# The order of TensorE's instructions behind the input projection, written in the source instead of planned

## Chip, cores and metric

The kernel runs on one core of one Trainium2 chip. The metric is the time of one execution on the device in microseconds (us), as the median of several runs; one more execution was recorded by the hardware profiler, and every row of the trace comes from that one.

## What is computed

One decoder block on 1024 tokens of width 1024, in float32. The state-space branch works in 8 chunks of 128 tokens, one after the other, because each chunk needs the state that the chunk before it left.

```
h = layer_norm(x)
xs, z, b, c, dt, glu, cgate = split(h @ w_in)            # 44 blocks of 128 columns, and dt
...
# state-space branch: 16 heads x 64, 2 groups, state 128, chunks of 128 tokens
y[chunk]  = (c b^T * decay) @ (x * dt)  +  c @ state * exp(cumsum)  +  d_skip * x
state     = state * chunk_decay  +  b^T @ (x * dt * decay_to_end)
y_ssm     = rms_norm(y * silu(z)) * ssm_norm_g
# convolution branch
y_conf    = silu(layer_norm(conv31(glu))) * silu(cgate)
out       = concat(y_ssm, y_conf) @ w_out
h1        = layer_norm(alpha * h + out + b_out)
result    = layer_norm(alpha * h1 + sigmoid(h1 @ w_ple_gate) * (p @ w_ple_proj))
```

## The kernel before

Every large matrix product is made of three passes: an operand is split into a rounded high part and the low rest (`split`, lines 117 to 120: ScalarE writes the high part, VectorE or GpSimd subtracts), and `three` (lines 122 to 125) issues low x high, high x low, high x high for each 128 rows of the contraction. So a line number of 123, 124 or 125 alone says little; the name of the output tile says which product it is: `ps` is the input projection, `pso` the output projection of the convolution branch, `pss` that of the state-space branch, `psg` the last gate.

The program has three stretches. In the first, the blocks of the input projection run (`inproj`), each in two halves of 24 matmuls: the blocks of the convolution branch, then those of x, B, C and z (`xbc_tile`, `z_tile`, the list `others`), then the norm over channels (`conf_norm`), the 8 gate blocks (`gate_tile`) and, behind them, the last two z blocks. Results that are needed by chunk go to memory (`xbc_d`, `z_d`, `mix_d`) and are read again.

In the second stretch the 8 chunks of the scan and the output projection of the convolution branch alternate. For chunk c, `prep` loads its inputs, takes the exponentials on ScalarE, turns x (`xtok`) and B and makes C B^T (`bps`) on TensorE, and weights them on VectorE. `chunk` does what needs the state (`yo`), what lies inside the chunk (`yd`) and the new state (`sp`), and gates with z on GpSimd. `mean_square` squares (ScalarE), adds up (GpSimd) and sums over channels with four tiny matmuls (`pr`). `conf_out` adds 48 matmuls (`pso`) to the residual. Meanwhile `out_weight` loads and splits the weights `wc` (convolution branch), `ws` (state-space branch) and `wg` (gate).

In the third stretch, for each 128 tokens, `out_proj` makes 48 matmuls (`pss`), a residual sum and a layer norm on VectorE and GpSimd, giving `r`; `turned` turns `r` with eight transposes (`pt`) and splits it into `hTH` and `hTL`; `gate` makes 48 matmuls (`psg`) from them, first of all one that reads `hTL`. The loop in the source is

```
    ready, last = out_proj(0, *ys.pop(0)), None
    for c in range(NT):
        if c + 2 < NT:
            ys.append(y_load(c + 2))
        following = out_proj(c + 1, *ys.pop(0)) if c + 1 < NT else None
        now = last or turned(c, ready)
        ahead = turned(c + 1, following) if c + 2 == NT else None
        gate(c, ready, *now)
        ready, last = following, ahead
```

What sets the order of the instructions on an engine: a planner (`schedule_with_timeline_sim=True`). It goes through a simulated execution and gives each engine, whenever it is free there, the instruction that is ready and stands earliest in the source. So the order of the source is a priority, and a later piece may overtake an earlier one that isn't ready. At run time each engine executes its list in that order; waits are semaphores. Tiles come from pools: a tag has a number of buffers (`BUFS`, lines 67 and 147), and a tile waits until a buffer of its tag comes free. Those that matter here are `y` (2 buffers: the last z blocks' results `zt`, the raw weights k = 3 and k = 7 of `wc`, and each chunk's `y`), `xb` (2: the inputs of a chunk), `E` and `M` (4 each, first held by the low part of the input of the input projection, which its last block still reads). In PSUM, `s` has 3 banks, `o` has 2, `b` one, and `cv` (with `xtok` and `pt`) one pair. All transfers are issued on SyncE's queue.

Of the kernel before, what the change touches and what calls it, by code (L numbers as in the profile page):

```python
# [46 lines left out]
def tile_block(ctx: ExitStack, tc: tile.TileContext, x, pT, wple, win, wdt, wout, wgate, vec, rows, heads, out):  # L47
    nc = tc.nc
    mm = nc.tensor.matmul

# [108 lines left out]
    def embed(half):  # L159
        for t in range(half * 4, half * 4 + 4):  # L160
            mu, rs = moments(xts[t], "0")
            if t in NORM_ACT:
                nm = small("nm0", 1)
                nc.gpsimd.tensor_scalar(out=nm, in0=mu, scalar1=rs, scalar2=-1.0, op0=ALU.mult, op1=ALU.mult)
                nc.scalar.activation(out=xts[t], in_=xts[t], func=AF.Identity, scale=rs, bias=nm)
            else:
                nc.vector.tensor_scalar(out=xts[t], in0=xts[t], scalar1=mu, scalar2=rs, op0=ALU.subtract, op1=ALU.mult)
        for k in range(NK):
            ps = obank("pst")
            for i in range(4):  # L170
                nc.tensor.transpose(out=ps[:, i * P:(i + 1) * P], in_=xts[half * 4 + i][:, k * P:(k + 1) * P], identity=ident)
            if k % 2 == 0:
                both = work("htmp", "ha" if k == 4 else "gt")
            tmp = both[:, k % 2 * 512:k % 2 * 512 + 512]
            nc.scalar.activation(out=tmp, in_=ps, func=AF.Identity, scale=v("lng", k), bias=v("lnb", k))
            hs = slice(half * 512, half * 512 + 512)
            nc.vector.tensor_copy(out=hH[k][:, hs].bitcast(F32R), in_=tmp)  # L177
            leng = nc.gpsimd if k in L_POOL else nc.vector
            leng.tensor_tensor(out=hL[k][:, hs].bitcast(F32R), in0=tmp, in1=hH[k][:, hs], op=ALU.subtract)  # L179
# [173 lines left out]
    def decays():  # L353
# [9 lines left out]
        psr = obank("psr")  # L363
        nc.tensor.transpose(out=psr[:, 0:P], in_=nacs, identity=ident)
        nc.vector.tensor_scalar(out=ar, in0=psr[:, 0:P], scalar1=-1.0, scalar2=None, op0=ALU.mult)
# [74 lines left out]

    def prep(c):

# [3 lines left out]
        for g in range(2):  # L446
# [3 lines left out]
            gg.append(gt)  # L450
        ea = slabs(work("ea", "u") if c == 0 else area("ea", "E"))
        for q in range(2):
            er = ea_d[c * HEADS:(c + 1) * HEADS, :].rearrange("(t q) l -> q t l", q=2)[q]
            nc.sync.dma_start(out=ea[q * HD:(q + 1) * HD], in_=er.unsqueeze(0).broadcast_to([HD, NK, P]))

        for h in range(HEADS):
            sl = gg[h // 8][:, h % 8, :]
            nc.scalar.activation(out=sl, in_=sl, func=AF.Exp, bias=col(nacs, c, h))
        xdt = work("xdt", "xd")
        xt = pair("xtok")  # L460
        for t in range(NK):
            nc.tensor.transpose(out=xt[:, t * P:(t + 1) * P], in_=xb[:, t, :], identity=ident)
        nc.vector.tensor_tensor(out=heads3(xdt), in0=heads3(xt), in1=col(dtok, c, 0, HEADS).unsqueeze(2).broadcast_to([P, HEADS, HD]), op=ALU.mult)
        xdd = work("xdd", "u") if c == 0 else area("xdd", "E")
        for h in range(HEADS):
            nc.scalar.activation(out=xdd[:, h * HD:(h + 1) * HD], in_=xdt[:, h * HD:(h + 1) * HD], func=AF.Copy, scale=col(dec, c, h))
        bps = bbank("bps")
        for g in range(2):
            nc.tensor.transpose(out=bps[:, g * P:(g + 1) * P], in_=xb[:, 8 + g, :], identity=ident)
            mm(bps[:, (2 + g) * P:(3 + g) * P], lhsT=xb[:, 8 + g, :], rhs=xb[:, 10 + g, :], start=True, stop=True)  # L470
# [9 lines left out]
    def z_load(c):  # L480
        sz = slabs(work("sz", "xd" if c == 0 else "u"))
        nc.sync.dma_start(out=sz, in_=z_d[c])
        return sz

    def chunk(c, sz, xb, gg, ea, xdt, xdd, btok):
        y = slabs(work("y", "y"))
        for g in range(2):

            ys = y[:, g * 4:g * 4 + 4, :]
            es = ea[:, g * 4:g * 4 + 4, :]  # L490
            if c:
                yo = bank("yo")
                for t in range(4):
                    j = g * 4 + t
                    mm(yo[:, t * P:(t + 1) * P], lhsT=state[:, j * P:(j + 1) * P], rhs=xb[:, 10 + g, :], start=True, stop=True)
                nc.vector.tensor_tensor(out=es, in0=slabs(yo, 4), in1=es, op=ALU.mult)
            yd = bank("yd")
            for h in range(8):
                q = h % 2
                t = h // 2  # L500
                hh = g * 8 + h
                mm(yd[q * HD:(q + 1) * HD, t * P:(t + 1) * P], lhsT=xdt[:, hh * HD:(hh + 1) * HD], rhs=gg[g][:, h, :], start=True, stop=True)
            for t in range(4):
                j = g * 4 + t
                nc.vector.scalar_tensor_tensor(out=y[:, j, :], in0=xb[:, j, :], scalar=v("dsk", j), in1=yd[:, t * P:(t + 1) * P], op0=ALU.mult, op1=ALU.add)
            if c:
                nc.gpsimd.tensor_tensor(out=ys, in0=ys, in1=es, op=ALU.add)
        nc.gpsimd.tensor_tensor(out=y, in0=y, in1=sz, op=ALU.mult)
        nc.sync.dma_start(out=y_d[c], in_=y)
        if c + 1 < NT:  # L510
            if c:
                nc.gpsimd.tensor_tensor(out=heads3(state), in0=heads3(state),
                                        in1=col(cdec, c, 0, HEADS).unsqueeze(2).broadcast_to([P, HEADS, HD]), op=ALU.mult)
            for g in range(2):
                sp = bank("sp")
                gs = slice(g * 512, g * 512 + 512)
                mm(sp, lhsT=btok[:, g * P:(g + 1) * P], rhs=xdd[:, gs], start=True, stop=True)
                if c:
                    nc.vector.tensor_tensor(out=state[:, gs], in0=state[:, gs], in1=sp, op=ALU.add)
                else:  # L520
                    nc.vector.tensor_copy(out=state[:, gs], in_=sp)
        return y, ea

    def mean_square(c, y, ea):

        sq = ea.rearrange("p (g t) l -> p g t l", g=2)
        nc.scalar.activation(out=sq, in_=y.rearrange("p (g t) l -> p g t l", g=2), func=AF.Square)
        nc.gpsimd.tensor_tensor(out=sq[:, :, 0:2, :], in0=sq[:, :, 0:2, :], in1=sq[:, :, 2:4, :], op=ALU.add)
        nc.gpsimd.tensor_tensor(out=sq[:, :, 0, :], in0=sq[:, :, 0, :], in1=sq[:, :, 1, :], op=ALU.add)
        pr = bbank("pr")  # L530
        for g in range(2):
# [7 lines left out]
    def mix_load(c):  # L539
        raw = slabs(work("mraw", "xb", L) if c == 0 else area("mraw", "M"))  # L540
        nc.sync.dma_start(out=raw, in_=mix_d[c])
        ha = work("ha", "ha")
        nc.sync.dma_start(out=ha, in_=ha_d[c])
        mH, mL = slabs(area("mH", "M")), slabs(area("mL", "M"))
        split(raw, mH, mL, nc.gpsimd if c else nc.vector)
        return mH.bitcast(F32R), mL.bitcast(F32R), ha

    def conf_out(c, mH, mL, ha):

        for n in range(2):  # L550
            nn = slice(n * 512, n * 512 + 512)
            ps = obank("pso")
            for k in range(NK):
                three(ps, mH[:, k, :], mL[:, k, :], wc[k][0][:, nn], wc[k][1][:, nn], k == 0, k == NK - 1)
            nc.vector.tensor_tensor(out=ha[:, nn], in0=ha[:, nn], in1=ps, op=ALU.add)
        nc.sync.dma_start(out=ha_d[c], in_=ha)

# [28 lines left out]
    def turned(c, r):  # L586
        hTH, hTL = (work(n, "xd" if c == NT - 1 else "u", L) for n in ("hTH", "hTL"))
        pt = pair("pt")
        for k in range(NK):
            nc.tensor.transpose(out=pt[:, k * P:(k + 1) * P], in_=r[:, k * P:(k + 1) * P], identity=ident)  # L590
        split(pt, hTH, hTL, nc.vector)
# [42 lines left out]
    conf_norm()  # L634
    ready = [prep(0)]
    while len(others) > LAST_Z:
        others.pop(0)()
    for j in range(NK):
        gate_tile(j, CG_TAGS[j])
    for f in others:  # L640
# [4 lines left out]
    mix = [mix_load(0)]  # L645
    szs = [z_load(0)]
    ready.append(prep(1))
    szs.append(z_load(1))
    ws = []
    for c in range(NT):  # L650
        done = chunk(c, szs.pop(0), *ready.pop(0))
        if c + 2 < NT:
            ready.append(prep(c + 2))
            szs.append(z_load(c + 2))
        mean_square(c, *done)
        if c + 1 < NT:
            mix.append(mix_load(c + 1))
        conf_out(c, *mix.pop(0))
        if c < 3:
            ws.append(out_weight(wout[c], area, "W", None, v("sng", c)))  # L660
    ys = []
    for k in range(3, NK):
        if k in (4, 6):
            ys.append(y_load(len(ys)))
        ws.append(out_weight(wout[k], area, "W" if k < 4 else "E" if k < 6 else "M", "xb" if k in (3, 5, 7) else None, v("sng", k)))
    gb = []
# [66 lines left out]
```

## Time and profile before

| | |
|---|---|
| median of 3 runs | 900.91 us (900.71 to 906.92) |
| the profiled execution: its own time | 904.0 us |
| the profiled execution: span, first to last instruction | 902.3 us |
| TensorE busy with matmuls | 866.7 us, 96% |
| VectorE / GpSimd / ScalarE busy | 638.4 us, 71% / 515.2 us, 57% / 393.5 us, 44% |
| TensorE's clock, mean granted share | 0.994 |
| data moved | 126.42 MB, 140 GB/s on average |

All rows are from the profiled execution. Times in the trace count from the start of its span. A matmul's duration there contains its way through the array, which overlaps the next matmul: where one follows the other, the distance from start to start is what it costs. "Idle before" in brackets is time in which the engine did nothing ahead of an instruction, with the instruction that ended it.

### The profile page before, as it was taken

To read this page: it belongs to the slowest core of one execution; us is meant where nothing else is said; L and a number is where in the kernel's file an instruction comes from. 1 tells how busy PE (TensorE), PEld (TensorE's weight loads), DVE (VectorE), ACT (ScalarE), POOL (GpSimd) and SP (SyncE) were. 2 spreads that over 40 slices of the span, in tenths; PEclk is the share of its full clock that TensorE was granted. 3 is DMA by queue.
4 is the path that set the end of the run, shared out by engine and by line. 5 is a ranking of instruction groups with operands and counts; after the bars stand their busy time and mean duration, and the time that the engine had idled before them with its cause. 6 is when DMAs were issued, how large, how long until landed. Compare 5 with 4: busy or idle time off the path is not lost. (4 is left out here: it accounts for less than half of the span.)

```text
span 902.3 us, 11012 instructions
## 1 busy us (share of the span) xinstructions
PE 866.7 (96%) x4141; PEld 705.7 (78%) x4141; DVE 638.4 (71%) x738; ACT 393.5 (44%) x649; POOL 515.2 (57%) x298
## 2 busy tenths in 40 slices
PE   6989999999999999999999999999999889999995
PEld 4757888888888888888788887777877668888885
DVE  7968993799999989894414604774664876666666
ACT  4632336767334456554584536754743421111001
POOL 2559829999832299997652345666666432222211
PEclk9999999999999999999999999999999899999999
DMA  9612423121221313234241879787787702222211
GB/s 339 252 44 97 176 84 117 30 94 46 94 84 58 94 46 129 70 94 117 70 141 47 249 232 338 268 305 224 250 274 262 291 24 94 94 94 93 71 47 70
DMA packets 67716, 126.42 MB, mean 140 GB/s; under 512 B 4176, under 2 KB 41552, under 8 KB 67664
## 3 DMA queue, kind: packets, MB, share of 16 engines
q1 hardware_dynamic: 67664, 125.73, 41.5%
q8 instruction: 32, 0.52, 0.2%
q14 instruction: 20, 0.16, 0.1%
HBM read 89.93 MB, written 35.78 MB: 139 GB/s over the span
## 5 line engine op out<-in xcount | busy, mean ns | idle before, releaser
L123 PE MATMUL ps<-hH,wl 128*128 128x512 f32 x704 | 274.4, 391 | 2.5 <-DVE hH L177 2.5
L124 PE MATMUL ps<-hL,wh 128*128 128x512 f32 x704 | 274.8, 391 | 1.1 <-DVE hL L179 1.1
L125 PE MATMUL ps<-hH,wh 128*128 128x512 f32 x704 | 274.3, 390 | 0.0
L291 DVE SCALAR_TENSOR_TENSOR pc<-u,vc,pc 128x1024 f32<-128x1024 f32 x174 | 223.7, 1285 | 3.5
L286 POOL TENSOR_TENSOR acc<-acc,prod 128x1024 f32<-128x1024 f32 x60 | 146.1, 2435 | 18.1 <-ACT acc L282 15.3
L123 PEld LDWEIGHTS ps<-hH,wl 128*128 128x128 f32 x704 | 131.9, 188 | 29.8 <-DVE hH L177 3.0
L124 PEld LDWEIGHTS ps<-hL,wh 128*128 128x128 f32 x704 | 132.3, 188 | 28.9 <-DVE hL L179 1.5
L125 PEld LDWEIGHTS ps<-hH,wh 128*128 128x128 f32 x704 | 132.3, 188 | 27.4 <-issue 0.2
L120 POOL TENSOR_TENSOR wl<-wraw,wh 128x1024 fp32r<-128x1024 f32 x44 | 110.2, 2504 | 72.6 <-PE ps L123 39.1
L132 POOL TENSOR_SCALAR ve<-mv 128x1 f32<-128x1 f32 x24 | 22.2, 926 | 122.1 <-DVE mv L612 86.9
L285 ACT ACTIVATE prod<-u,vc 128x1024 f32<-128x1024 f32 x60 | 69.0, 1153 | 46.8 <-POOL acc L286 36.7
L119 ACT CAST wh<-wraw 128x1024 fp32r<-128x1024 f32 x44 | 46.2, 1049 | 67.8 <-DMA wraw<-in_win_dram 42.5
L380 DVE SCALAR_TENSOR_TENSOR pc<-xin,vc,pc 128x512 f32<-128x512 f32 x72 | 53.5, 747 | 5.9 <-ACT pc L247 3.4
L123 PE MATMUL pss<-woh,yL 128*128 128x512 f32 x128 | 51.7, 404 | 5.7 <-DVE r L581 3.5
L123 PE MATMUL pso<-woh,mL 128*128 128x512 f32 x128 | 51.8, 407 | 2.9 <-POOL mL L120 1.9
L123 PE MATMUL psg<-woh,hTL 128*128 128x512 f32 (+1 forms) x136 | 52.3, 385 | 1.1 <-DVE hTL L120 1.1
L125 PE MATMUL psg<-woh,hTH 128*128 128x512 f32 (+1 forms) x136 | 52.0, 382 | 0.0
L125 PE MATMUL pso<-woh,mH 128*128 128x512 f32 x128 | 51.9, 407 | 0.0
L124 PE MATMUL pso<-wol,mH 128*128 128x512 f32 x128 | 51.7, 404 | 0.0
L124 PE MATMUL psg<-wol,hTH 128*128 128x512 f32 (+1 forms) x136 | 51.6, 380 | 0.0
L124 PE MATMUL pss<-wol,yH 128*128 128x512 f32 x128 | 50.9, 398 | 0.0
L125 PE MATMUL pss<-woh,yH 128*128 128x512 f32 x128 | 50.9, 398 | 0.0
(183 smaller groups left out, 1390.4 us busy)
## 6 DMA issues: line engine op xcount, KB each, us to landing
wraw<-in_win_dram SPq DMA_DIRECT2D x44, 512.0 KB, 3.7
gt<-acs_d SPq DMA_DIRECT2D x16, 512.0 KB, 5.2
wor<-in_wout_dram SPq DMA_DIRECT2D x16, 512.0 KB, 6.8
xbc_d<-cacc SPq DMA_DIRECT2D x12, 512.0 KB, 3.4
xb<-xbc_d SPq DMA_DIRECT2D x8, 768.0 KB, 6.3
xt<-in_x_dram SPq DMA_DIRECT2D x8, 512.0 KB, 8.9
ple_d<-pl SPq DMA_DIRECT2D x8, 512.0 KB, 3.8
ha_d<-xt SPq DMA_DIRECT2D x8, 512.0 KB, 4.8
```

The source lines that it names most:

```text
L119: nc.scalar.copy(out=h.bitcast(F32R), in_=src)
L120: leng.tensor_tensor(out=l.bitcast(F32R), in0=src, in1=h, op=ALU.subtract)
L123: mm(ps, lhsT=ll, rhs=rh, start=first, stop=False)
L124: mm(ps, lhsT=lh, rhs=rl, start=False, stop=False)
L125: mm(ps, lhsT=lh, rhs=rh, start=False, stop=last)
L132: eng.tensor_scalar(out=ve, in0=var, scalar1=EPS, scalar2=None, op0=ALU.add)
L285: nc.scalar.activation(out=pr, in_=u[:, i:i + L], func=AF.Copy, scale=v("ccw", j * KC + i))
L286: nc.gpsimd.tensor_tensor(out=acc, in0=acc, in1=pr, op=ALU.add)
L291: nc.vector.scalar_tensor_tensor(out=pc if i + 1 < KC else acc, in0=u[:, i:i + L], scalar=v("ccw", j * KC + i), in1=pc, op0=ALU.mult, op1= ...
L380: nc.vector.scalar_tensor_tensor(out=pc, in0=xin[:, o + j:o + j + 512], scalar=v("scw", i * 4 + j), in1=pc, op0=ALU.mult, op1=ALU.add)
```

## The change

Three things change; the arithmetic stays, apart from work whose result was never read.

1. A list `pinned` is filled once, behind the input projection, and never emptied. From then on each matmul and each transpose gets an edge to the instruction traced just before it on TensorE (`keep_in_program_order`), which fixes their order in TensorE's list to that of the source; it is no wait for the earlier one's result. All matmuls and transposes of the program go through the two wrappers. The other engines' orders are still the planner's.
2. `conf_out` becomes a generator with 16 steps of three matmuls, and `chunk` is cut into `from_state`, `inside` (per group), `advance` and `gated`. The loop over chunks now writes an order: what needs the state, two steps, the next chunk's `prep`, two steps, `inside` of group 0, two steps, of group 1, two steps, `advance`, the mean square of the chunk before, eight steps.
3. Chunk 0 (without its gate) and `prep` of chunk 1 stand in the source between the gate blocks and the last two z blocks; its tile `y` is taken there. Some tiles get other tags (`mraw` leaves `M` for `W`, the last chunk's `mH` and `mL` go to `gt`). The `ea` of chunk 0 and the `xdd` of chunk 7 are no longer made.

The loop of the third stretch is not edited.

```diff
-    mm = nc.tensor.matmul
+    pinned = []
+
+    def on_pe(ins):
+
+        if pinned:
+            tc.keep_in_program_order(ins)
+
+    def mm(*args, **kw):
+        on_pe(nc.tensor.matmul(*args, **kw))
+
+    def transpose(**kw):
+        on_pe(nc.tensor.transpose(**kw))
...
-        ea = slabs(work("ea", "u") if c == 0 else area("ea", "E"))
-        for q in range(2):
+        ea = slabs(work("ea", "u") if c == 1 else area("ea", "E")) if c else None
+        for q in range(2 if c else 0):
...
-        xdd = work("xdd", "u") if c == 0 else area("xdd", "E")
-        for h in range(HEADS):
+        xdd = (work("xdd", "u") if c < 2 else area("xdd", "E")) if c + 1 < NT else None
+        for h in range(HEADS if c + 1 < NT else 0):
...
+    def from_state(c, xb, ea):
+
         for g in range(2):
             es = ea[:, g * 4:g * 4 + 4, :]
-            if c:
-                yo = bank("yo")
...
+            yo = bank("yo")
             for t in range(4):
                 j = g * 4 + t
+                mm(yo[:, t * P:(t + 1) * P], lhsT=state[:, j * P:(j + 1) * P], rhs=xb[:, 10 + g, :], start=True, stop=True)
+            nc.vector.tensor_tensor(out=es, in0=slabs(yo, 4), in1=es, op=ALU.mult)
+        if c + 1 < NT:
+            nc.gpsimd.tensor_tensor(out=heads3(state), in0=heads3(state),
+                                    in1=col(cdec, c, 0, HEADS).unsqueeze(2).broadcast_to([P, HEADS, HD]), op=ALU.mult)
...
-        raw = slabs(work("mraw", "xb", L) if c == 0 else area("mraw", "M"))
+        raw = slabs(work("mraw", "gt") if c == 0 else area("mraw", "W"))
...
-        mH, mL = slabs(area("mH", "M")), slabs(area("mL", "M"))
+        mH, mL = (slabs(area(n, "M") if c + 1 < NT else work(n, "gt")) for n in ("mH", "mL"))
...
                 three(ps, mH[:, k, :], mL[:, k, :], wc[k][0][:, nn], wc[k][1][:, nn], k == 0, k == NK - 1)
-            nc.vector.tensor_tensor(out=ha[:, nn], in0=ha[:, nn], in1=ps, op=ALU.add)
-        nc.sync.dma_start(out=ha_d[c], in_=ha)
+                if k == NK - 1:
+                    nc.vector.tensor_tensor(out=ha[:, nn], in0=ha[:, nn], in1=ps, op=ALU.add)
+                    if n:
+                        nc.sync.dma_start(out=ha_d[c], in_=ha)
+                yield
...
         for k in range(NK):
-            nc.tensor.transpose(out=pt[:, k * P:(k + 1) * P], in_=r[:, k * P:(k + 1) * P], identity=ident)
+            transpose(out=pt[:, k * P:(k + 1) * P], in_=r[:, k * P:(k + 1) * P], identity=ident)
         split(pt, hTH, hTL, nc.vector)
...
     for j in range(NK):
         gate_tile(j, CG_TAGS[j])
+
+    def own(c, y, xb, gg, ea, xdt, xdd, btok):
+        for g in range(2):
+            inside(c, g, y, xb, gg, ea, xdt)
+            yield
+
+    y = slabs(work("y", "y"))
+    for _ in own(0, y, *ready):
+        pass
+    advance(0, *ready[4:])
+    ready = prep(1, *prep_load(1))
     for f in others:
         f()
...
+    conf = conf_out(0, *mix_load(0))
+
+    def turn(n):
+        for _ in range(n):
+            next(conf)
+
+    sq = gated(0, y, None, z_load(0))
+    szs = [z_load(1)]
+    loaded = prep_load(2)
     ws = []
-    for c in range(NT):
...
+    pinned.append(True)
+    for c in range(1, NT):
+        y = slabs(work("y", "y"))
+        xb, gg, ea, xdt, xdd, btok = ready
+        steps = own(c, y, *ready)
+        from_state(c, xb, ea)
+        turn(2)
+        if c + 1 < NT:
+            ready = prep(c + 1, *loaded)
+        turn(2)
+        next(steps)
+        turn(2)
+        next(steps)
+        turn(2)
+        if c + 1 < NT:
+            advance(c, xdd, btok)
+        mean_square(c - 1, sq)
+        following = mix_load(c)
         if c + 2 < NT:
-            ready.append(prep(c + 2))
-            szs.append(z_load(c + 2))
-        mean_square(c, *done)
+            loaded = prep_load(c + 2)
+        sq = gated(c, y, ea, szs.pop(0))
         if c + 1 < NT:
-            mix.append(mix_load(c + 1))
-        conf_out(c, *mix.pop(0))
-        if c < 3:
-            ws.append(out_weight(wout[c], area, "W", None, v("sng", c)))
+            szs.append(z_load(c + 1))
+        if c < 4:
+            ws.append(out_weight(wout[c - 1], area, "W", None, v("sng", c - 1)))
+        turn(8)
+        conf = conf_out(c, *following)
+    turn(10)
+    mean_square(NT - 1, sq)
+    turn(6)
     ys = []
```

`inside`, `advance` and `gated` hold the lines that `chunk` had for them, and `prep` is cut into `prep_load` (the transfers and the exponentials) and the rest.

## Rows read from the trace of the kernel before

**Rows 1.** The page, busy time, share of the span and instructions of each engine:
```profile
PE 866.7 (96%) x4141; PEld 705.7 (78%) x4141; DVE 638.4 (71%) x738; ACT 393.5 (44%) x649; POOL 515.2 (57%) x298
```

**Rows 2.** Stretches: length, busy us (instructions) of PE PEld DVE ACT POOL, PEclk, DMA, GB/s:
```profile
100.00:200.00 100.00, 100.00 (x445) 82.86 (x444) 80.10 (x82) 56.03 (x67) 76.47 (x38) 1.00 0.31 102
545.80:698.80 153.00, 145.45 (x874) 116.04 (x873) 93.50 (x149) 84.22 (x240) 99.34 (x61) 1.00 0.83 276
703.90:710.70 6.80, 5.49 (x12) 3.80 (x12) 6.80 (x5) 2.08 (x2) 6.80 (x3) 0.50 0.96 354
731.80:879.00 147.20, 147.18 (x666) 121.13 (x667) 96.58 (x122) 19.99 (x25) 37.11 (x32) 1.00 0.22 79
```

**Rows 3.** TensorE's waits in the whole trace: total us, times, longest:
```profile
PE pss L123 <- DVE r L581: 3.5, 2, 2.3
...
PE bps L469 <- DVE cbm L474: 2.4, 1, 2.4
PE pss L123 <- DVE ha L555: 2.3, 1, 2.3
PE pr L532 <- POOL ea L529: 1.9, 2, 1.7
PE pso L123 <- POOL mL L120: 1.9, 1, 1.9
...
PE psg L123 <- DVE hTL L120: 1.1, 2, 0.6
...
PE pso L123 <- DVE mL L120: 1.0, 1, 1.0
...
PE xtok L462 <- DMA xb<-xbc_d: 0.3, 1, 0.3
```

**Rows 4.** Timeline of TensorE, start of the second stretch: start, duration, instruction:
```profile
543.27 1.97 PE L502 MATMUL yd<-gt,xdt 128*64 128x128 f32 x32
547.42 0.50 PE L123 MATMUL pso<-woh,mL 128*128 128x512 f32 x1 [1.01 <-DVE mL L120]
...
556.66 1.04 PE L462 MATMUL xtok<-ident,xb 128*128 128x128 f32 x8
...
560.97 1.05 PE L495 MATMUL yo<-xb,state 128*128 128x128 f32 x8
```

**Rows 5.** Timelines of SyncE's queue, ScalarE and GpSimd there: the last raw weight:
```profile
545.25 0.38 SPq L387 DMA_DIRECT2D z_d<-zt  x1
...
548.77 0.43 SPq L422 DMA_DIRECT2D wor<-in_wout_dram  x1
...
552.03 1.05 ACT L119 CAST woh<-wor 128x1024 fp32r<-128x1024 f32 x1 [1.23 <-DMA wor<-in_wout_dram]
...
553.21 2.39 POOL L120 TENSOR_TENSOR wol<-wor,woh 128x1024 fp32r<-128x1024 f32 x1 [3.59 <-ACT woh L119]
```

**Rows 6.** The page, DMA issues: KB each, median us from issue to landing:
```profile
xb<-xbc_d SPq DMA_DIRECT2D x8, 768.0 KB, 6.3
```

**Rows 7.** The chain of work that ended last, 868 to 884 us, in order:
```profile
869.66 0.23 PE psg L123
...
879.00 0.89 PE pt L590 x8
879.97 1.02 ACT hTH L119
881.01 1.24 DVE hTL L120
882.29 0.50 PE psg L123
```

**Rows 8.** Timeline of VectorE behind the last `pss` matmul:
```profile
869.70 0.75 DVE L581 SCALAR_TENSOR_TENSOR r<-pss,rsm,r 128x512 f32<-128x512 f32 x1 [1.24 <-PE pss L125]
...
871.46 1.28 DVE L567 SCALAR_TENSOR_TENSOR r<-r,mv,gb 128x1024 f32<-128x1024 f32 x1
873.51 1.28 DVE L568 SCALAR_TENSOR_TENSOR r<-r,rs,gb 128x1024 f32<-128x1024 f32 x1 [0.77 <-POOL rs L134]
```

More of the change, by code (lines that the diff above doesn't have):

```diff
@@ L170, in embed @@
             for i in range(4):
-                nc.tensor.transpose(out=ps[:, i * P:(i + 1) * P], in_=xts[half * 4 + i][:, k * P:(k + 1) * P], identity=ident)
+                transpose(out=ps[:, i * P:(i + 1) * P], in_=xts[half * 4 + i][:, k * P:(k + 1) * P], identity=ident)
             if k % 2 == 0:
@@ L363, in decays @@
         psr = obank("psr")
-        nc.tensor.transpose(out=psr[:, 0:P], in_=nacs, identity=ident)
+        transpose(out=psr[:, 0:P], in_=nacs, identity=ident)
         nc.vector.tensor_scalar(out=ar, in0=psr[:, 0:P], scalar1=-1.0, scalar2=None, op0=ALU.mult)
@@ L439, in heads3, with prep_load @@
         return a.rearrange("p (h d) -> p h d", d=HD)
-    def prep(c):
+    def prep_load(c):
         xb = slabs(work("xb", "xb", 12 * P), 12)
@@ L458, in prep @@
             nc.scalar.activation(out=sl, in_=sl, func=AF.Exp, bias=col(nacs, c, h))
+        return xb, gg, ea
+    def prep(c, xb, gg, ea):
         xdt = work("xdt", "xd")
@@ L461, in prep @@
         for t in range(NK):
-            nc.tensor.transpose(out=xt[:, t * P:(t + 1) * P], in_=xb[:, t, :], identity=ident)
+            transpose(out=xt[:, t * P:(t + 1) * P], in_=xb[:, t, :], identity=ident)
         nc.vector.tensor_tensor(out=heads3(xdt), in0=heads3(xt), in1=col(dtok, c, 0, HEADS).unsqueeze(2).broadcast_to([P, HEADS, HD]), op=ALU.mult)
-        xdd = work("xdd", "u") if c == 0 else area("xdd", "E")
-        for h in range(HEADS):
+        xdd = (work("xdd", "u") if c < 2 else area("xdd", "E")) if c + 1 < NT else None
+        for h in range(HEADS if c + 1 < NT else 0):
             nc.scalar.activation(out=xdd[:, h * HD:(h + 1) * HD], in_=xdt[:, h * HD:(h + 1) * HD], func=AF.Copy, scale=col(dec, c, h))
@@ L468, in prep @@
         for g in range(2):
-            nc.tensor.transpose(out=bps[:, g * P:(g + 1) * P], in_=xb[:, 8 + g, :], identity=ident)
+            transpose(out=bps[:, g * P:(g + 1) * P], in_=xb[:, 8 + g, :], identity=ident)
             mm(bps[:, (2 + g) * P:(3 + g) * P], lhsT=xb[:, 8 + g, :], rhs=xb[:, 10 + g, :], start=True, stop=True)
@@ L480, in z_load @@
     def z_load(c):
-        sz = slabs(work("sz", "xd" if c == 0 else "u"))
+        sz = slabs(work("sz", "xd" if c < 2 else "u"))
         nc.sync.dma_start(out=sz, in_=z_d[c])
         return sz
-    def chunk(c, sz, xb, gg, ea, xdt, xdd, btok):
-        y = slabs(work("y", "y"))
+    def from_state(c, xb, ea):
         for g in range(2):
-            ys = y[:, g * 4:g * 4 + 4, :]
             es = ea[:, g * 4:g * 4 + 4, :]
-            if c:
-                yo = bank("yo")
[L493 to L502, printed above, removed]
+            yo = bank("yo")
@@ L503, in chunk @@
             for t in range(4):
                 j = g * 4 + t
-                nc.vector.scalar_tensor_tensor(out=y[:, j, :], in0=xb[:, j, :], scalar=v("dsk", j), in1=yd[:, t * P:(t + 1) * P], op0=ALU.mult, op1=ALU.add)
+                mm(yo[:, t * P:(t + 1) * P], lhsT=state[:, j * P:(j + 1) * P], rhs=xb[:, 10 + g, :], start=True, stop=True)
[3 more added lines that the diff above has]
+                                    in1=col(cdec, c, 0, HEADS).unsqueeze(2).broadcast_to([P, HEADS, HD]), op=ALU.mult)
@@ new lines, in inside @@
+    def inside(c, g, y, xb, gg, ea, xdt):
+        yd = bank("yd")
+        for h in range(8):
+            q = h % 2
+            t = h // 2
+            hh = g * 8 + h
+            mm(yd[q * HD:(q + 1) * HD, t * P:(t + 1) * P], lhsT=xdt[:, hh * HD:(hh + 1) * HD], rhs=gg[g][:, h, :], start=True, stop=True)
+        for t in range(4):
+            j = g * 4 + t
+            nc.vector.scalar_tensor_tensor(out=y[:, j, :], in0=xb[:, j, :], scalar=v("dsk", j), in1=yd[:, t * P:(t + 1) * P], op0=ALU.mult, op1=ALU.add)
+        if c:
+            ys = y[:, g * 4:g * 4 + 4, :]
+            nc.gpsimd.tensor_tensor(out=ys, in0=ys, in1=ea[:, g * 4:g * 4 + 4, :], op=ALU.add)
@@ L506, in chunk, with advance @@
+    def advance(c, xdd, btok):
+        for g in range(2):
+            sp = bank("sp")
+            gs = slice(g * 512, g * 512 + 512)
+            mm(sp, lhsT=btok[:, g * P:(g + 1) * P], rhs=xdd[:, gs], start=True, stop=True)
             if c:
-                nc.gpsimd.tensor_tensor(out=ys, in0=ys, in1=es, op=ALU.add)
+                nc.vector.tensor_tensor(out=state[:, gs], in0=state[:, gs], in1=sp, op=ALU.add)
+            else:
+                nc.vector.tensor_copy(out=state[:, gs], in_=sp)
@@ L508, in chunk, with gated @@
+    def gated(c, y, ea, sz):
         nc.gpsimd.tensor_tensor(out=y, in0=y, in1=sz, op=ALU.mult)
         nc.sync.dma_start(out=y_d[c], in_=y)
[L510 to L521, printed above, removed]
@@ L522, in chunk @@
-        return y, ea
-    def mean_square(c, y, ea):
+        if ea is None:
+            ea = slabs(area("sq", "E"))
         sq = ea.rearrange("p (g t) l -> p g t l", g=2)
@@ L529, in mean_square @@
         nc.gpsimd.tensor_tensor(out=sq[:, :, 0, :], in0=sq[:, :, 0, :], in1=sq[:, :, 1, :], op=ALU.add)
+        return sq
+    def mean_square(c, sq):
         pr = bbank("pr")
@@ L634, in tile_block @@
     conf_norm()
-    ready = [prep(0)]
+    ready = prep(0, *prep_load(0))
     while len(others) > LAST_Z:
@@ L639, in tile_block @@
         gate_tile(j, CG_TAGS[j])
+    def own(c, y, xb, gg, ea, xdt, xdd, btok):
+        for g in range(2):
+            inside(c, g, y, xb, gg, ea, xdt)
[5 more added lines that the diff above has]
+    ready = prep(1, *prep_load(1))
     for f in others:
@@ L644, in tile_block @@
     wc = [out_weight(wout[NK + k], *regs[k], "y" if k % 4 == 3 else None) for k in range(NK)]
[L645 to L648, printed above, removed]
-    ws = []
-    for c in range(NT):
-        done = chunk(c, szs.pop(0), *ready.pop(0))
+    conf = conf_out(0, *mix_load(0))
[5 more added lines that the diff above has]
+    loaded = prep_load(2)
+    ws = []
+    pinned.append(True)
[16 more added lines that the diff above has]
+        following = mix_load(c)
         if c + 2 < NT:
-            ready.append(prep(c + 2))
-            szs.append(z_load(c + 2))
-        mean_square(c, *done)
+            loaded = prep_load(c + 2)
+        sq = gated(c, y, ea, szs.pop(0))
         if c + 1 < NT:
-            mix.append(mix_load(c + 1))
-        conf_out(c, *mix.pop(0))
-        if c < 3:
-            ws.append(out_weight(wout[c], area, "W", None, v("sng", c)))
+            szs.append(z_load(c + 1))
[6 more added lines that the diff above has]
+    turn(6)
     ys = []
@@ L664, in tile_block @@
             ys.append(y_load(len(ys)))
-        ws.append(out_weight(wout[k], area, "W" if k < 4 else "E" if k < 6 else "M", "xb" if k in (3, 5, 7) else None, v("sng", k)))
+        ws.append(out_weight(wout[k], area, "W" if k < 4 else "E" if k < 6 else "M", None if k == 4 else "xb", v("sng", k)))
     gb = []
```

## The prediction

> **What bounds the kernel now.** I read the busy times first: TensorE works 96% of the span, no other engine over 71% [rows 1]. So the time is TensorE's work plus its gaps, and the change removes no work of TensorE: it can only close gaps or open them. The stretches say where gaps are [rows 2]. From 100 to 200 us TensorE is never idle, and from 731.8 to 879 it lacks 0.02 us of 147.2; a matmul costs 147.2 / 666 = 0.221 us there, so a step of three costs 0.66. From 545.8 to 698.8, where the chunks run, 7.5 us of 153 are missing, and behind that up to 731.8 TensorE stands again, once at half its clock. Third comes the table of waits [rows 3], which names each gap: in the chunks 2.4 (`bps`), 1.9 (`pr`), 1.9 and 1.0 (`pso`) and 0.3 (`xtok`), together 7.5; at the passage to the third stretch 3.5 + 2.3 (`pss`) and about 0.5 (`psg`). The rest of the waits is early and not touched. These two sums are all that a better order can win.
>
> **The third stretch, which the edit doesn't show.** `pinned` is never emptied, so the order of the source also binds `out_proj`, `turned` and `gate`. In the source that is: 48 `pss` of block c+1, eight `pt` of block c, 48 `psg` of block c. The first `psg` reads `hTL`, which takes the transposes, then ScalarE, then VectorE. Rows 7 have this chain with nothing hiding it: `pt` ends at 879.89, ScalarE needs 1.02, VectorE 1.24, and `psg` starts at 882.29, 2.40 later [rows 7]. Today the planner hides it: in 147 us that hold six such turns it loses 0.02 us [rows 2], because it puts `pt` amid the `pss`. With the fixed order nothing may slip in between. Moreover VectorE isn't free: behind the last `pss` it does the residual, the statistics and L567, which stand earlier in the source. On the scale of the last block, `pss` ends about 869.66 [rows 7], `pt` at 870.55, the high part at 871.65, but L567 runs from 871.46 to 872.74 [rows 8]; then 1.24 for `hTL`, so `psg` starts at about 874.0: a gap of 3.5. Bounds are 2.4 (VectorE free) and 3.5; I take 3.5, because VectorE is given L567 as soon as the statistics end, just ahead of the high part. This happens for c = 1 to 5, five times: 17.5 us (12.0 to 17.5). For c = 0 it falls among the waits at the passage, which I leave as they are, below.
>
> Block 6 is worse and single. The source has `pt` of block 7 ahead of the `psg` of block 6, and it needs `r` of block 7, whose last `pss` has just ended. `r` is ready when L568 ends, 874.79, against 870.55, where `pt` of block 6 ends [rows 7, 8]: a gap of 4.2. Today the planner puts 40 of the 48 `psg` there and loses 0.6 to `hTL` (1.1 less the 0.5 at the passage [rows 3]). Net 3.6 us (3.3 to 4.5). `psg` of block 6 and 7 then run through.
>
> **The clock.** After the 2.3 us wait of `pss` on `ha` the granted clock was 0.50 from 703.9 to 710.7, which is 1.2 instead of 2.4 GHz; only 12 matmuls started in these 6.8 us, where 31 would in the dense stretch [rows 2, 3]. Waits of 2.4 and 1.9 us went by without a fall. So gaps just over 2 us sometimes cost the clock, and gaps of 3.5 and 4.2 are longer than any of these. I take it that five of the six fall, each for the 6.8 us of the row. Half speed for 6.8 us costs 3.4, less the end of the gap that it overlaps, 3.0: 15 us (0 to 24, the last with a seventh fall at the start of the chunks).
>
> **The chunks.** The six waits in the chunks are of the kind that a spread order hides: `bps` stands 2.4 us because the one bank of `b` isn't read yet, `pr` because GpSimd isn't through; in the new order two steps of `pso` lie between pieces, and `pr` belongs to the chunk before. All but the first (the 1.0, part of the start below) go: -6.5 (0 at worst). The cover is the eight steps, 5.3 us, behind the state's update, and 1.3 between the other pieces. What could be late instead is `xb`: two buffers, so the transfer for chunk c+2 starts when chunk c is done and must land within about 11 us (two steps, `sp`, `pr`, eight steps, `yo`, two steps, less VectorE's reading); it takes 6.3 at the median [rows 6], and one wait of 0.3 is all that there was [rows 3]. I put 1 us for seven chunks (0 to 7). The tags that change relax `M` (`mraw` no longer takes one of four), which is behind the 1.9 for `mL`; the 16 small ScalarE instructions and two transfers left out are on no path.
>
> By the Trainium skill ("Perfetto Trace Analysis", section "Identifying the Most-Contended Engine") the share of weight loads, not of matmuls, says how near TensorE is to its limit. By that share the chunks stand further off: 116.04 of 153.00 against 82.86 of 100 [rows 2], so 13 us and not 7.5 would be open; the sum would fall by some 6 us. I stay with the waits, as the chunks hold small matmuls that load fewer weights per time.
>
> **The start of the chunks.** Chunk 0 (547.42 - 543.27 - 1.01 = 3.1) and the second `prep` (1.0 for `xtok` [rows 4], some 1.5 with `bps`) move ahead of the last z blocks, so these end 4.6 us later, about 547.9; that is work moved, not added. But today these 3.1 us cover part of the way to the first `pso`, 4.15 us from 543.27 to 547.42, since `mL` must wait for buffers that the z block still reads. Now only `yo` covers it, 2 x 1.05 [rows 4]: a wait of 2.1. Next the buffers of `y`: chunk 0's `y` takes one of the two before the z blocks and holds it until all of z is stored, read again and multiplied. Both last `zt` and the raw weights k = 3 and 7 then share the other, if buffers are given in the order of the source. Today the last `zt` is stored at 545.25, the raw weight behind it is issued at 548.77 and split by 555.60 [rows 5]: 3.5 and 6.8 us. With the shift of 4.6, the buffer is free at 553.4, weight 3 is ready at 560.2, weight 7 at 567.0. TensorE reaches weight 3 at about 552.0 + 3 steps + 1.5 = 555.5 and waits 4.7; then one step, `inside` (1.0 a group [rows 4]), two steps, `inside`, a step: 564.9, and it waits 2.1 for weight 7. The planner could have gone on with other pieces here; the fixed order can't. Together 2.1 + 4.7 + 2.1 = 8.9, less the 1.0 of today: +7.9. At best the buffers come otherwise and only the first wait stays, +1.1; at worst the two transfers take the 6.3 that `xb` takes at the median [rows 6] and not 3.3: +14.
>
> **The passage.** From 698.8 to 731.8 the limits are weights that are split on VectorE and GpSimd, both busy all of the 6.8 us at half clock [rows 2]. Their order isn't edited; `E` and `M` come free somewhat earlier. I leave it at 0: between -9.7 (3.5 + 2.3 + 0.5 and 3.4 of clock gone) and +3.5 (the gap of c = 0 on top).
>
> **The sum.** 17.5 + 3.6 + 15 - 6.5 + 1 + 7.9 + 0 = +38.5 on the profiled execution's own 904.0, which is 942.5. That execution lies 3.1 above the median of the runs, 900.91; so 939.
>
> **Rivals.** (1) The clock holds, as it did at the gap of 2.4: the same gaps without the 15, 924. For it: three of four gaps near 2 us kept the clock; against: the new ones are longer. (2) The start costs more: transfers of 6.3 us add 6, and two waits of over 4 us lose the clock for 3 each: 951. For it: the data engines are 83% busy there [rows 2]. (3) The order of the third stretch doesn't become what the source says, and `pt` stays amid the `pss`: then nothing of 17.5 + 3.6 + 15 is paid. What is left turns on one price, the start: as long as it stays under the 16.2 us that the chunks and the passage can give back, the kernel is faster; with +1.1 it would be 901 - 15 = 886. Against: the wrapper has all matmuls and transposes, and nothing ends it. (4) Small prices everywhere (start 1.1, passage -9.7, gaps of 2.4, no fall): 12 + 3.3 + 1.1 - 6.5 - 9.7 = 0, no change, 901.
>
> **How the numbers follow.** Forecast 939: 0.50. Clock holds, 924: 0.22. Start costs more, 951: 0.15. Small prices, 901: 0.07. Third stretch not bound, 886: 0.06. A change of 1% is about what a measurement of this kernel can tell from none; so faster 0.06, same 0.07, slower 0.87. The range leaves out (3) and (4) and reaches around (1) and (2): 912 to 956, with the start at its best below and most falls of the clock above.
>
> **What will show it.** In the third stretch `psg` should wait for `DVE hTL` about 3.5 us at each of five blocks, `pt` once about 4 us for `r`, and the granted clock fall behind most of these. In the chunks `bps`, `pr` and `pso` should no longer wait on VectorE and GpSimd; near 550 to 567 `pso` should wait for the weights of k = 3 and 7 (`wor`, `wol`). I am wrong if `pt` still lies within a run of `pss`, if the clock stays, or if the chunks end much more than 7 us sooner.

## The result, and the profile after

The changed kernel takes 956.68 us (median of 4 runs, 953.34 to 960.59) against 903.59 for the kernel before in the same comparison: a ratio of 1.056, 95% interval 1.052 to 1.061, slower (the two medians as they stand give 1.059, inside that interval). The forecast was 939 and its range 912 to 956; on the 900.91 that it started from, the ratio gives 951.5, inside the range and beside the 951 of rival (2). One execution of experiment e5 ran at about half speed from start to end, 1786.83 us, and stands outside its ratio. The profiled execution has a span of 958.9 us against 902.3.

I cut both traces at the same four events (end of the last `ps`, first `pss`, first `psg`, end of the last `psg`). The three stretches between them are called the chunks, the passage and the third stretch. First those of the kernel before, by the columns of [rows 2]:

```profile
543.30:698.80 155.50, 147.91 (x907) 118.04 (x907) 94.54 (x149) 86.14 (x243) 101.23 (x61) 1.00 0.83 274
698.80:731.80 33.00, 26.77 (x110) 20.70 (x108) 28.55 (x25) 12.15 (x12) 15.75 (x8) 0.90 0.55 205
731.80:893.80 162.00, 161.40 (x752) 133.49 (x752) 106.01 (x135) 22.58 (x29) 38.97 (x34) 1.00 0.22 78
```

Then those of the changed kernel:

```profile
553.00:718.30 165.30, 148.16 (x860) 115.59 (x858) 89.64 (x139) 76.17 (x203) 99.86 (x61) 0.94 0.76 239
718.30:753.00 34.70, 25.32 (x105) 19.78 (x105) 24.34 (x26) 11.96 (x12) 18.35 (x10) 0.88 0.60 220
753.00:950.40 197.40, 175.55 (x752) 143.57 (x752) 102.12 (x131) 21.07 (x29) 35.34 (x31) 0.92 0.17 62
```

The third stretch issues the same 752 matmuls, takes 35.4 us longer, and its clock is 0.92 instead of 1.00. The chunks take 9.8 longer although chunk 0 lies ahead of them now, and begin 9.6 later. The passage is 1.8 longer (1.7 by the rounded cuts of these lines). Together this is the 56.6 us between the spans.

TensorE's waits in the whole trace, which answer to [rows 3]:

```profile
PE psg L57 <- DVE hTL L131: 23.4, 6, 6.3
PE pso L57 <- ACT woh L130: 8.7, 1, 8.7
...
PE pt L60 <- DVE r L594: 4.9, 2, 4.7
PE pss L57 <- DVE r L607: 2.7, 1, 2.7
PE sp L57 <- DVE y L523: 2.6, 3, 2.0
PE sp L57 <- ACT cg L307: 2.2, 1, 2.2
PE xtok L60 <- DMA xb<-xbc_d: 1.9, 1, 1.9
...
PE pso L57 <- POOL wol L131: 1.7, 1, 1.7
PE pss L57 <- DVE ha L579: 1.5, 1, 1.5
```

All wrapped matmuls now have line 57, so the tile's name is what to read. The waits for `cbm`, `ea` and `mL` have gone from the list; `hTL`, `r` and `woh` stand in their place.

One turn of the third stretch, block 1, in TensorE's timeline:

```profile
777.71 1.03 PE L60 MATMUL pt<-ident,r 128*128 128x128 f32 x8
782.17 0.50 PE L57 MATMUL psg<-woh,hTL 128*128 128x512 f32 x1 [3.43 <-DVE hTL L131]
```

and what VectorE did meanwhile:

```profile
779.66 1.32 DVE L593 SCALAR_TENSOR_TENSOR r<-r,mv,gb 128x1024 f32<-128x1024 f32 x1
780.91 1.21 DVE L131 TENSOR_TENSOR hTL<-pt,hTH 128x1024 fp32r<-128x1024 f32 x1
```

The transposes stand behind all 48 `pss`, the gap is 3.43, and L593 (L567 before) goes ahead of `hTL`, as the prediction had it from [rows 8]. The five gaps of blocks 1 to 5 are 3.42 or 3.43 each; that of block 0 is 6.29, since VectorE still splits gate weights there. In block 6 the second set of transposes waits for `r`:

```profile
924.78 1.94 PE L60 MATMUL pt<-ident,r 128*128 128x128 f32 x8 [4.68 <-DVE r L594]
```

At the end of each of these gaps, or within 0.5 us of it, the granted clock is at the lower level, 1.2 GHz: two such stretches, and the long one near the start of the chunks:

```profile
782.50:785.90 3.40, 3.40 (x10) 2.61 (x9) 0.81 (x1) 1.04 (x1) 0.00 (x0) 0.51 0.03 8
809.90:813.30 3.40, 3.02 (x7) 2.44 (x8) 1.52 (x2) 1.04 (x1) 0.00 (x0) 0.51 0.21 83
560.70:574.40 13.70, 5.73 (x24) 3.89 (x25) 3.98 (x4) 6.07 (x8) 6.17 (x4) 0.50 0.66 241
```

The start of the chunks, in the chain of work that ended last (the rows that aren't TensorE's):

```profile
554.65 7.43 DMA z_d<-zt
562.08 0.02 issue
562.10 3.77 DMA wor<-in_wout_dram
565.87 0.02 issue
565.89 1.05 ACT woh L130
...
567.07 2.35 POOL wol L131
```

The last z block's store ends at 562.08, and only then is the raw weight k = 3 of `wc` issued, in the buffer that the store has freed; TensorE stands for it, 8.7 and 1.7 us.

### The profile page after: what moved, and what is told of

The parts are those of the page before. It is cut to its first block, busy times and chain, and to the rows that moved or that the text cites. A ratio compares the mean times of both kernels' runs of the same rounds, so it can differ in the third digit from the quotient of the medians.

```text
span 958.9 us, 10964 instructions
## 1 busy us (share of the span) xinstructions
PE 888.9 (93%) x4141; PEld 719.3 (75%) x4141; DVE 632.6 (66%) x738; ACT 392.9 (41%) x635; POOL 512.8 (53%) x298
## 4 chain that ended last, share of the span: by engine, by line
PE 76%; DMA 10%; DVE 7%; ACT 3%; issue 2%; POOL 1%; SPq 1%; POOLq 0%; DVEq 0%; ACTq 0%
PE ps L57 47%; PE psg L57 11%; PE pss L57 7%; PE pso L57 4%; PE psp L57 3%; DMA wor<-in_wout_dram 2%; DVE r L593 1%; DMA wor<-in_wgate_dram 1%; PE sp L57 1%; DMA xb<-xbc_d 1%; DMA yraw<-y_d 1%; DMA ha_d<-ha 1%; DMA y_d<-y 1%; ACT acc L308 1%; DMA ea<-ea_d 1%
## 5 line engine op out<-in xcount | busy, mean ns | idle before, releaser
L57 PE MATMUL psg<-woh,hTL 128*128 128x512 f32 (+1 forms) x136 | 58.1, 427 | 23.4 <-DVE hTL L131 23.4
L57 PE MATMUL pso<-woh,mL 128*128 128x512 f32 x128 | 55.5, 434 | 9.4 <-ACT woh L130 8.7
L634 DVE TENSOR_TENSOR gt<-gt,pl 128x512 f32<-128x512 f32 (+1 forms) x17 | 11.2, 660 | 74.2 <-ACT gt L633 74.2
L57 PE MATMUL psg<-woh,hTH 128*128 128x512 f32 (+1 forms) x136 | 56.5, 416 | 0.0
L57 PE MATMUL psg<-wol,hTH 128*128 128x512 f32 (+1 forms) x136 | 56.1, 413 | 0.0
L131 POOL TENSOR_TENSOR wol<-wor,woh 128x1024 fp32r<-128x1024 f32 x12 | 29.8, 2484 | 45.7 <-ACT woh L130 28.6
L469 ACT ACTIVATE gt<-gt,nacs 128x128 f32<-128x128 f32 x128 | 39.3, 389 | 34.4 <-DMA gt<-acs_d 34.3
```

The costliest lines, as they stand in the source:

```text
L57: on_pe(nc.tensor.matmul(*args, **kw))
L131: leng.tensor_tensor(out=l.bitcast(F32R), in0=src, in1=h, op=ALU.subtract)
L634: nc.vector.tensor_tensor(out=gt[:, nn], in0=gt[:, nn], in1=pl[:, nn], op=ALU.mult)
```

## The experiments

Times are medians beside runs of the kernel before on the same chip (904.5 to 905.7 there; 903.6 for the changed kernel). The table has the cuts from above, in us of the profiled execution: end of the last `ps`, then the lengths of the chunks, the passage and the third stretch.

| kernel | median | ratio to before | last `ps` | chunks | passage | third |
|---|---|---|---|---|---|---|
| before | - | 1 | 543.3 | 155.6 | 32.9 | 162.0 |
| changed | 956.7 | 1.056 (1.052 to 1.061) | 552.9 | 165.4 | 34.7 | 197.4 |
| e1 third released | 928.4 | 1.026 (1.024 to 1.029) | 552.5 | 163.3 | 34.9 | 168.5 |
| e2 no edges | 918.7 | 1.016 (1.014 to 1.018) | 552.1 | 152.1 | 35.6 | 168.4 |
| e3 gaps filled | 944.5 | 1.044 (1.042 to 1.047) | 553.1 | 158.4 | 34.8 | 186.0 |
| e4 y elsewhere | 955.2 | 1.056 (1.053 to 1.059) | 552.0 | 160.3 | 34.1 | 198.4 |
| e5 before, third pinned | - | 1.042 (1.034 to 1.050) | 541.1 | 154.5 | 39.3 | 196.3 |
| e6 third written | 921.9 | 1.017 (1.011 to 1.023) | 551.9 | 163.2 | 34.8 | 161.8 |
| e7 start freed | 911.3 | 1.006 (1.002 to 1.009) | 553.1 | 151.6 | 36.2 | 161.8 |
| e8 chunk 0 behind | 917.6 | 1.012 (1.005 to 1.018) | 541.3 | 168.5 | 35.2 | 161.8 |
| e9 chunk 0 later | 905.7 | 1.000 (0.997 to 1.003) | 549.0 | 154.2 | 33.0 | 161.7 |

In e5 and e8 chunk 0 lies behind the last `ps`, as in the kernel before; in the others it lies ahead. The changed kernel, e1, e3 and e6 have the same order up to the first `pss`, on TensorE and on the other engines, and their chunks take 158.4 to 165.4: a difference under 7 us in that column alone says nothing.

**e1: the third stretch released.**

```diff
     turn(6)
+    pinned.clear()
     ys = []
```

> The changed kernel with the list of pinned instructions emptied between the second and the third stretch, so that the planner orders the third stretch again. Theory A (the third stretch loses 35 us: five gaps of 3.4, one of 4.7, and the clock behind them, because the order of the source leaves nothing to do while hTL is made): the third stretch takes about 170 us again instead of 206, the waits for DVE hTL of 3.4 are gone, about 918 (913 to 923). Theory B (the third stretch is slow because the second ends late with its weights and stands in their way, whoever orders it): 945 or more.

The third stretch falls from 197.4 to 168.5, and the waits for `hTL` but for one of 2.9. So its time is made by its order: theory B, that the late end of the chunks stands in its way, is out. 918 wasn't reached: 162 doesn't come back. (The 206 and 170 of the expectation run to the end of the kernel; by that cut the stretch is now 177.) The rest is in the table of waits:

```profile
PE pss L57 <- POOL yL L131: 8.0, 6, 1.4
```

The planner, free again, gave this source another order than in the kernel before: `pt` stands half a block later against `pss`, and in six blocks a `pss` waits 1.1 to 1.4 us for `yL`. With it 24 `pss` have moved ahead of the first `psg`, so that the third stretch has 729 matmuls and not 752: the 6.5 us that it takes more than before understate these waits.

**e2: no edges at all.**

```diff
-    pinned.append(True)
```

> The changed kernel with nothing pinned at all: its source order, its generator, its tags and the moved chunk 0, but all order the planner's. Theory A (fixed order is what costs, at the start of the chunks too, since nothing may overtake a matmul that waits for a weight): below the run with only the third stretch released, by the 8.7 and 1.7 us of waiting for the weight and some clock, so 900 to 910. Theory C (the start of the chunks is late because of the moved chunk 0 and its buffer, pinned or not): the same as with the third stretch released, 915 to 921.

The third stretch is that of e1, waits for `yL` included; the chunks take 152.1 instead of 163.3. No wait for `woh` is left. So at the start the fixed order costs what overtaking would have saved, as theory A has it. The time itself, 918.7, lies in theory C's range, but both ranges were set against an e1 that came out ten higher; C forecast no difference to e1, and it is 9.7. The 900 to 910 of theory A was too low, because 6.4 of the third stretch and 9 us ahead of the last `ps` stay.

**e3: the gaps filled.** 14 matmuls (19 at the end) whose result nobody reads are added between `pt` and `psg`.

```diff
+    def fill(n):
+        ps = bbank("fill")
+        for _ in range(n):
+            mm(ps, lhsT=ws[0][0][:, 0:P], rhs=ws[0][0][:, 0:512], start=True, stop=True)
...
         now = last or turned(c, ready)
+        if last is None:
+            fill(14 if c + 2 < NT else 19)
```

> The changed kernel, fully pinned, with 14 matmuls of 128x512 on data at hand (their result is not read) between the transposes and the psg of blocks 0 to 5, and 19 between the two sets of transposes at the end: added work that fills the gaps. Theory A (of the 35 us about 14 are the clock that falls behind each gap): the gaps stay filled, the clock stays at 1.00 in the third stretch, and the time falls by 10 to 16 although 103 matmuls are added: 941 to 947. Theory D (the clock in the third stretch costs nothing of note, or falls for another reason): 955 to 962.

TensorE's timeline in block 1, and the third stretch:

```profile
769.87 1.03 PE L60 MATMUL pt<-ident,r 128*128 128x128 f32 x8
770.65 3.43 PE L57 MATMUL fill<-woh 128*128 128x512 f32 x14
774.36 0.50 PE L57 MATMUL psg<-woh,hTL 128*128 128x512 f32 x1 [0.27 <-DVE hTL L131]
```

```profile
746.20:932.20 186.00, 184.27 (x841) 150.81 (x841) 102.33 (x131) 21.22 (x28) 35.55 (x31) 0.99 0.18 66
```

The gap is as long as before, but worked through: the clock stays (0.99 against 0.92), and the third stretch is 11.4 us shorter with 89 matmuls more (the 14 of block 0 lie in the passage, where a gap of 3.1 and a fall of 3.4 us behind it are left). This separates the two parts of the cost: 197.4 - 161.8 = 35.6 for the order (e6), 11 to 14 of it the clock, the rest the gaps, 5 x 3.42 + 4.68 = 21.8.

**e4: the y of chunk 0 in a buffer of `ha`.**

```diff
-    y = slabs(work("y", "y"))
+    y = slabs(work("y", "ha"))
     for _ in own(0, y, *ready):
```

> The changed kernel with one tag changed: the y of chunk 0 takes a buffer of ha instead of one of y, so that the last z results and the two raw weights have both buffers of y again. Theory A (TensorE's wait of 8.7 + 1.7 for a split weight near 560 comes from the buffer that chunk 0 holds): that wait goes but for 1 to 2 us, with the clock behind it, 941 to 949. Theory E (the weight is late because transfers are slow there, the data engines being 80% busy): the wait stays, 953 to 958.

The time says theory E, but the cause is another. TensorE's waits from 545 to 600 us:

```profile
PE pr L57 <- POOL sq L548: 8.4, 1, 8.4
PE pso L57 <- POOL wol L131: 2.5, 1, 2.5
```

The wait for the weight is gone (2.5 is left), so the buffer was its cause; a wait of the same length has come behind it, for the mean square of chunk 0. In the chain GpSimd gates with z at 569.50 and again, for the next chunk, at 574.14, and then adds the squares, until 578.5:

```profile
569.50 3.34 POOL y L541
...
574.14 2.35 POOL y L541
576.49 1.23 POOL sq L547
577.72 0.07 issue
577.79 0.74 POOL sq L548
```

In the fixed order the four `pr` stand ahead of eight steps of `pso` that were ready.

**e5: the kernel before, third stretch alone pinned** (the wrappers of the change, filled ahead of the first `pss`; nothing else).

```diff
+    pinned.append(True)
     ready, last = out_proj(0, *ys.pop(0)), None
```

> The kernel before, with only the matmuls and transposes of the third stretch kept in the order of the source (the edges begin ahead of its first pss); chunks, tags and the rest are as they were. Theory A (the order of the third stretch by itself costs what was predicted: gaps of 3.4 and one of 4.2, and the clock): 29 to 37 us on top of the kernel before, 934 to 942, with the waits for hTL and a fall of the clock behind most. Theory B (it costs only because the second stretch ended late): under 910.

The profile of this run is of the execution that is left out; the lengths in the table come from one execution more.

> The kernel before with the third stretch kept in the order of the source, once more, for a profile at the usual clock. Theory A: the third stretch from the first psg to the last takes 190 to 200 us instead of 162, with waits for hTL of 2.4 to 3.5 in blocks 1 to 5, one for r of 4 to 5, and the clock at 0.5 behind most. Theory B (no cost of its own): 162 to 170.

The ratio, 1.042, is 38 us, one more than theory A's range; the second profile has the third stretch at 196.3, its waits for `hTL` 20.6 in six turns and one of 4.7 for `r`. Order alone does it, with the chunks as they were.

```profile
PE psg L57 <- DVE hTL L131: 20.6, 6, 3.4
...
PE pt L60 <- DVE r L579: 4.7, 1, 4.7
```

**e6: the third stretch written out.** `turned` of block c is called between the two groups of `out_proj` of block c+1, that of block 7 in `gate` of block 6 ahead of k = 5 of its second half. All edges stay.

```diff
         for g in range(2):
+            if g and amid:
+                amid()
...
+            following = out_proj(c + 1, *ys.pop(0), amid=lambda: now.append(turned(c, ready)))
+        if c + 2 == NT:
+            gate(c, ready, *now[0], amid=lambda: ahead.append(turned(c + 1, following)))
```

> The changed kernel, still pinned throughout, with the source of the third stretch rewritten so that the transposes of block c stand between the two groups of out_proj of block c+1, and those of block 7 behind 39 of the 48 psg of block 6. Theory A (not the edges cost but the order that they fix): the gaps go, the third stretch takes about 165 to 170 us, at most the time of the run with it released, 918 to 929. Theory F (fixed edges cost by themselves, since nothing can give way to small delays): 935 or more.

161.8 us, clock 1.00, the 162.0 of the kernel before to 0.2:

```profile
749.80:911.60 161.80, 161.47 (x753) 133.28 (x751) 106.20 (x135) 22.60 (x29) 39.52 (x34) 1.00 0.22 78
```

Edges cost nothing by themselves in this stretch; theory F is out. A fixed good order is even better than the planner's in e1 by 6.7.

**e7: e6, and the start freed**: the `y` of e4, and the mean square of chunk 0 in the loop of chunk 2.

```diff
         turn(2)
+        if c == 2:
+            mean_square(0, sq0)
...
-        mean_square(c - 1, sq)
+        if c > 1:
+            mean_square(c - 1, sq)
+        else:
+            sq0 = sq
```

> The run with the third stretch written, and besides the y of chunk 0 in a buffer of ha and the mean square of chunk 0 one chunk later. Theory A (the start loses 8.3 + 1.7 to the weight behind the buffer, and with the buffer alone 8.4 to the mean square, which hangs on the same store of z and is fixed just behind): both go together with the clock behind them, 9 to 13 us less than the run with the third stretch written, 907 to 918. Theory E (the next thing is late as well, transfers being what limits the start): 0 to 4 us less.

10.5 us less than e6, as theory A has it: buffer and mean square were two waits one behind the other. The first repair alone (e4) showed nothing of it; the second alone was not run. The chunks fall from 163.2 to 151.6, and the clock stays there:

```profile
553.10:704.70 151.60, 142.76 (x861) 111.75 (x859) 93.67 (x140) 76.20 (x202) 101.11 (x61) 1.00 0.80 261
```

**e8: e6, with chunk 0 and `prep` of chunk 1 behind the z blocks** (the block of five lines moved behind `for f in others`, tag `y`).

> The run with the third stretch written, with chunk 0 and prep of chunk 1 behind the last z blocks in the source, as in the kernel before, pinned from the loop on, with the tag y for chunk 0. Theory A (the early chunk 0 takes the buffer and leaves the start uncovered): the waits for the weight shrink to 0 to 3 us, chunk 0 covers the way to the first pso again, 8 to 14 us less than the run with the third stretch written, 906 to 920. Theory G (the fixed loop itself makes the start late): within 4 us of it.

4.3 us less than e6, between the theories by that difference (the 906 to 920 of theory A was set wider, and 917.6 lies in it). The last `ps` ends 10.6 earlier, but the chunks, which hold chunk 0 again, take 168.5; its waits for weights are still 8.9 in four pieces:

```profile
PE pso L57 <- POOL wol L131: 5.4, 2, 3.4
PE pso L57 <- ACT woh L130: 3.5, 2, 2.1
```

This run doesn't separate the early chunk 0 from the fixed order, since one thing in it is not as in the kernel before: its `y` of chunk 0 is still taken ahead of the weights in the source, there it is taken behind them. So the raw weights k = 3 and 7 still share one buffer, as the chain shows: k = 7 is issued when GpSimd has split k = 3.

```profile
559.65 3.31 POOL wol L131
562.96 0.02 issue
562.98 7.38 DMA wor<-in_wout_dram
```

That the fixed order is needed for the wait is shown by e2, which keeps the early chunk 0 and its buffer and has no wait for `woh`.

**e9: e7, with chunk 0 between the last two z blocks, and `pt` of block 0 a quarter of `out_proj` later.**

```diff
+    others.pop(0)()
     y = slabs(work("y", "ha"))
     for _ in own(0, y, *ready):
```

> The run with the start freed, with chunk 0 and prep of chunk 1 between the last two z blocks instead of ahead of both, and the transposes of block 0 a quarter of out_proj later. Theory A (chunk 0 amid the gate blocks costs 2.2 of waiting and the clock behind it; pt of block 0 stands 7.5 for r): 4 to 7 us less than the run with the start freed, 904 to 908, as fast as the kernel before. Theory H (these waits only move): 909 to 913.

905.67, ratio 1.000 (0.997 to 1.003): 5.6 less than e7. The last `ps` ends 4 us earlier, without the waits of 0.7 for `cg` and 2.0 for `y` that e7 had ahead of it, the passage is 3.2 shorter, and the chunks 2.6 longer (a new wait of 2.7 for `mL`). With these repairs the written order is as fast as the planned one, and no run was faster.

## Why the prediction was right, and where its sizes were off

The time lies in the range and beside rival (2), not beside the forecast: the third stretch came out as forecast, the chunks cost 17 us more.

**The third stretch** was forecast at 17.5 + 3.6 + 15 = 36.1 and measured 35.4. The gaps were forecast at 3.5, five times, and are 3.42; the bound that I took, VectorE first at L567, is what the trace shows. Block 6's gap was forecast at 4.2 and is 4.68. e5 shows it on the kernel before, e6 shows that the order and not the edges is the cause.

**The clock** was forecast at 15 and is 13.8 by what e6 leaves beside the gaps; the trace of the changed kernel agrees, where TensorE works 28.7 us of the third stretch at the lower level, and half of that is 14.4. The 11.4 of e3 is less because a fall behind block 0 is left there. The sum holds, its parts don't, and that is luck: all six gaps lost the clock and not five, and the fall behind block 0, which wasn't counted, reaches 5.7 us into the stretch; but four of the falls lasted 3.4 us, half of the 6.8 in [rows 2].

**The chunks** are the term that was mis-sized: -6.5 + 1 + 7.9 = +2.4 was forecast, +19.4 came (9.6 at the last `ps`, 9.8 behind it). By the traces some 11.8 of it is more idle time of TensorE (2.2 ahead of the last `ps`; 17.1 against 7.6 in the chunks) and some 7.9 is half of the 15.8 us that it works at the lower clock; the clock stood at 0 in the sum. Four things make it up. Chunk 0 amid the gate blocks was priced as work moved, 4.6, and moves the last `ps` by 9.6: TensorE waited 2.2 for a bank that ScalarE still had to read into `cg`, and lost the clock behind it for 3.4 us; e9, which has neither there, still ends the last `ps` 5.7 later than the kernel before, so the work moved is 5.7. The wait at the start was forecast at 2.1 for `mL` + 4.7 + 2.1 for the raw weights k = 3 and 7, and is 8.7 + 1.7 for k = 3 alone; the sums are close by luck. Weight 3 is later than forecast because the last z block is stored 4.8 later and its store takes 7.4 and not 3.5. The mechanism was right, the buffer (e4), but behind it stood the mean square, which the prediction didn't see, so that freeing the buffer alone gives nothing. The clock fell there for 13.7 us, which I had only in the upper bound. And the fixed order paid for delays of 1 to 3 us that differ between executions: `xb` 1.9, `sp` 2.6 in three, with a fall behind the first and behind the longest `sp`, 2.0. The -6.5 itself came true: the waits for `cbm`, `ea` and `mL` are gone.

**The passage** was left at 0 and is +1.8; block 0's gap fell into it, as forecast. That it came out so near 0 may be luck: in e5, with the chunks as they were, the passage is 6.4 longer, and no run separates what made it shorter in the changed kernel.

**The rivals.** That the clock holds is out by the falls behind every gap. That the start costs more came, and the time is this rival's, 951; the clock was lost there as it says, but of its slower transfers only the store of z was one, the weight's own took 3.8. That the third stretch isn't bound is out, and with gaps of 3.4 that lost the clock so is the one of small prices. By the share of weight loads, the rule of the Trainium skill ("Perfetto Trace Analysis", section "Identifying the Most-Contended Engine"), 13 us stood open in the chunks. The shortest chunks, those of e7, have 151.6 + 4.6 of moved chunk 0 = 156.2 (157.3 with 5.7) against 155.6, so none of the runs here shows such a gain. Why executions with the same order take 158.4 to 165.4 for the chunks stays open; between e3 and the changed kernel, the two ends, 3.7 of the 7.0 is idle time of TensorE, and the clock is at the lower level for 13.7 and 20.5 us.

## What to carry over

An order that is fixed in the source binds all that follows until it is ended: look for the stretch that the edit doesn't show, and ask of each short chain (transposes, copy, subtract) what the planner had put into it. Here a gap on the engine that bounds the kernel cost its length and the clock behind it: of the third stretch's 35 us, 11 to 14 were the clock. When a wait is freed and the time stays, look for the next wait in the same place before giving up the cause: here two waits, one behind the other, showed only when both were taken away.

## What the hardware showed beyond that

Six of six gaps of 3.4 to 4.7 us in the third stretch had the lower clock at their end or within 0.5 us of it, and so had the six of e4 and of e5's second profile, while in e3 gaps of 0.3 had not. Shorter gaps go either way: in the kernel before, one of 2.3 had it and one of 2.4 hadn't; in the chunks of the changed kernel a fall began 1.1 us behind one of 1.9 and 1.5 us behind one of 2.0. Work that nobody reads, put into the gaps, made the kernel 12 us faster (944.5 against 956.7). And the same order of instructions, on every engine, took 158 to 165 us for the chunks in four executions, where the kernel before, whose order the planner had made, shows 154.5 and 155.6 in its two.
